# Plain float32 products in place of three split passes for the filters' and long convolutions' transforms

## The chip, the cores and the metric

The kernel runs on one core of a Trainium2 chip. The metric is the device time of one execution in microseconds (us). Three runs of the kernel before took 3001.47, 3002.57 and 3002.89 us, median 3002.57 us. The trace comes from one further, profiled execution, whose own time was 2998.99 us.

A core has a matrix engine (TensorE, PE in the rows; its weight loads are PEld), VectorE (DVE), ScalarE (ACT), GpSimd (POOL) and a queue that issues transfers (SP). Each engine works through its own list of instructions in order.

## The reference, cut to what matters

Two transformer-like blocks run one after the other on a sequence of 512 positions and 1024 channels. The first block has two branches, a linear recurrence (branch A) and a Hyena operator (branch B), then a mixture of 16 experts; the second has four kinds of attention and a feed-forward part. The change is in the Hyena filters and in their long convolutions:

```python
def hyena_filters(L, w1, b1, w2, b2, w3, freq):
    ...
    h = jnp.sin(freq[1] * (h @ w2.astype(f32) + b2.astype(f32)))
    h = (h @ w3.astype(f32)).reshape(L, HYENA_ORDER, 2, HYENA_WIDTH)
    ...
    return h * decay[:, None, None, :]

def fftconv(u, k, bias):
    L = u.shape[1]
    U = jnp.fft.rfft(u, n=2 * L, axis=1)
    K = jnp.fft.rfft(k, axis=0)
    y = jnp.fft.irfft(U * K[None], n=2 * L, axis=1)[:, :L]
    return y + u * bias.astype(jnp.float32)
    ...
        z = v.astype(f32)
        for n, gate in enumerate((x1, x2)):
            k = bidir_kernel(filt[:, n, 0], filt[:, n, 1])
            z = gate.astype(f32) * fftconv(z, k, filt_bias[l, n])
        y_b = z.astype(dt) @ w_b_out[l]
```

## The kernel before, in words

The kernel passes these stages, with the times of the trace: the first norm and the gate of branch A (0 to 58 us); the recurrence of branch A, in whose gaps the Hyena filters are made and transformed (58 to 268 us, `recurrence`, `make_filters`); the output product of branch A (268 to 316 us); branch B (316 to 607 us, `branch_b`); the merge of the branches (607 to 705 us); the experts (705 to 1650 us), paced by their weights' transfers; the second block (1650 to 2997 us).

A float32 operand that goes into a matrix product is split in two: `hi`, a copy rounded to the type float32r (made by ScalarE), and `lo`, the rest, `x - hi` (made by VectorE with a subtraction, L155 in `split`). The product is then three float32r passes into the same PSUM tile (`mm3`, L163 to L165): hi by hi, lo by hi, hi by lo. A matrix product of the experts, the transposes (operand `ident`) and a few small ones take plain float32 operands, with no split.

The transforms use a table `dft` of 2048 columns: 16 blocks of 128 by 128, cosines and sines of a Fourier transform at half-odd frequencies; 8 blocks serve the forward transform and 8 the inverse. It is split once, at the start, into `dft_h` and `dft_l`. A channel quarter `q` (256 of the 1024 channels) and an order `n` (0 or 1) make one filter and one long convolution, eight of each.

- `filters(n, q)` makes a filter's time samples: four products of 512 columns (tiles `fps`), times the decay (`fb`, L1282), each split into `sdh`, `sdl`.
- `filters.transforms` sends them through `transform`: six PSUM tiles of two products each (12 products of 128 by 128 by 256 columns), sums and differences on VectorE (`so`, `sa`, `K`), and stores the spectrum `K` to DRAM.
- `long_conv` transforms the signal (`uh`, `ul`; 8 products), multiplies it with the spectrum (`pq`, `U`, L1358 to L1361), forms sums and differences, and splits the four result tiles into `Yh`, `Yl`. `inverse` then makes 8 products into two tiles `cps`.
- After order 0, `gated` multiplies the result with a gate (`z`, L1411) and splits it into the next `uh`, `ul`. After order 1, `last` transposes the result back and multiplies it into `x` (L1425). `to_operand` makes the first `uh`, `ul` from transposed tiles (L1341, L1342).

So there are 96 products in the filters' transforms, 64 in the signals' forward and 64 in the inverse transforms, three passes each. Between them stand the projections of the input (`acc` from `hh`, `hl` and `wh`, `wl`; 24 passes of 512 columns each, with one split of the weights, `wl`, 128 by 1024 on VectorE, per projection).

The program's steps are written in an order given by two strings (`STEPS_A` for the recurrence, filters and transforms; `STEPS_B` for branch B: c is a projection, u an operand, L a long convolution, M its inverse, G a gate's projection). A scheduler then interleaves the instructions of neighbouring steps in each engine's list; the tiles' buffer counts (`CFG1`) limit how far it goes.

Of the kernel before, what the change touches and what calls it, by code (L numbers as in the profile page):

```python
# [846 lines left out]
CFG1 = dict(acc=3, c=2, f=3, hA=0, lA=1, gh=0, gl=1, hB=0, lB=1, kh=0, kl=1, xh=0, xl=1, sh=0, sl=1, yh=0, yl=1, wl=1, rA=1, rX=1, bl=0, tA=5, tB=5, cv=9, U=3, Y=4, th=5, fA='vvvv', fB='vvvv', gB='vvvv', hB2='vvvv', xg=1, K=1, zh=0, zl=1)  # L847
# [82 lines left out]
def body_t1(c, A):  # L930
# [87 lines left out]
    dft_h = dp.tile([128, 2048], F32R, name="dft_h")  # L1018
    dft_l = dp.tile([128, 2048], F32R, name="dft_l")
    HS = dp.tile([128, T], F32R, name="HS")  # L1020
    HS0 = dp.tile([128, 256], F32R, name="HS0")
    with pool("filt") as fp:
        softplus_cols(c, fp, sp, p1[:, 176:192], 16, -4.0)
        nc.vector.tensor_scalar(spd, sp, 2.0, None, op0=OP.mult)
        filter_mlp(c, A, fp, ps_f, dft_h, dft_l, HS, HS0)
    c.kd = c.dram.tile([8, 128, 4, T], F32, name="filters_dram")
    with pool("lru", 2, side="right") as lp:
        recurrence(c, A, h, proj, lp, ps_c, ps_f, hb, sp, spd, quarter, dft_h, dft_l, HS, HS0)
    with pool("lru2", 2, side="right") as lp:
        branch_a(c, A, h, proj, lp)  # L1030
    with pool("hy", 2, side="right") as bp:
        branch_b(c, A, h, proj, ps_c, ps_f, bp, dft_h, dft_l)
# [40 lines left out]
def filter_mlp(c, A, fp, ps_f, dft_h, dft_l, HS, HS0):  # L1073
# [38 lines left out]
def recurrence(c, A, h, proj, lp, ps_c, ps_f, hb, sp, spd, quarter, dft_h, dft_l, HS, HS0):  # L1112
# [7 lines left out]
    filters = make_filters(c, A, ps_f, t, lp, ws2, dft_h, dft_l, HS, HS0)  # L1120
# [86 lines left out]
def make_transform(c, ps_f, t, dft_h, dft_l, NT, st2):  # L1207
# [40 lines left out]
def make_filters(c, A, ps_f, t, bp, ws, dft_h, dft_l, HS, HS0):  # L1248
    nc = c.nc
    NT = CFG1["tA"]  # L1250
    transform = make_transform(c, ps_f, t, dft_h, dft_l, NT, CFG1["fA"])

    def filters(n, q):
# [10 lines left out]
        sh, sl = t("sdh", 1, F32R, 8 * Q), t("sdl", 1, F32R, 8 * Q)  # L1264
        r = lambda a: a.rearrange("p (g i n) -> p g i n", g=2, i=4)
        for i in range(4):
# [570 lines left out]
```

## Time and profile before

| quantity | value |
|---|---|
| median of three runs | 3002.57 us |
| profiled execution, own time | 2998.99 us |
| its span, first to last instruction | 2997.2 us |
| PE busy | 2789.5 us (93%) |
| PEld busy (weight loads, beside PE) | 1851.5 us (62%) |
| DVE busy | 1595.7 us (53%) |
| ACT busy | 966.0 us (32%) |
| POOL busy | 177.6 us (6%) |
| mean granted TensorE clock | 0.976 of full speed |

The shares are means over stages with different limits, so they say nothing by themselves about one stage. The end of a matrix product in the trace is modelled: one product's duration is longer than its distance to the next one, and this distance is what a product costs in a dense stream. The same holds, less strongly, for VectorE.

A plain float32 product is recorded as two instructions: the 56 plain products at L1736 in pairs of experts, of 128 by 128 by 512 columns, are 112 records.

### The profile page before, as it was taken

The numbers are of one execution on the slowest core, as the hardware profiler recorded it, in microseconds if no ns is written. First come the engines' busy times: TensorE is split into PE (matmuls) and PEld (weight loads), VectorE is DVE, ScalarE is ACT, GpSimd is POOL, SyncE is SP. The second block draws the span as 40 slices with busy tenths as digits, with TensorE's granted clock in tenths as the row PEclk, the third lists the DMA queues.
The fourth block names the chain that finished last, engine by engine and source line by source line (L and its number), as shares of the span: only waits on it lengthen the run. The fifth ranks groups of instructions, "written<-read, shape, count | busy, mean of one in ns | idle before, by whom it ended". The sixth has DMA issues, their size and how long they took to land.

```text
span 2997.2 us, 35639 instructions
## 1 busy us (share of the span) xinstructions
PE 2789.5 (93%) x13524; PEld 1851.5 (62%) x13524; DVE 1595.7 (53%) x3205; ACT 966.0 (32%) x1629; POOL 177.6 (6%) x150
## 2 busy tenths in 40 slices
PE   8898988699999999998988899899999999999998
PEld 7677876575333333333333676688888776688887
DVE  7997599954122222222211889663435788654345
ACT  6774333231000000000000358442223367433224
POOL 0000000000000000000000223200000233100000
PEclk9999998899999999999999899999999999999999
DMA  4344322258999999999999233232222323232324
GB/s 158 130 141 165 120 95 75 98 199 353 417 421 420 420 421 421 421 421 421 420 421 392 89 94 86 64 105 98 94 96 97 119 76 83 76 103 94 99 92 134
DMA packets 136356, 617.94 MB, mean 206 GB/s; under 512 B 17423, under 2 KB 31575, under 8 KB 84600
## 3 DMA queue, kind: packets, MB, share of 16 engines
q1 hardware_dynamic: 136184, 615.65, 54.4%
q8 instruction: 107, 1.75, 0.2%
q14 instruction: 65, 0.53, 0.1%
HBM read 582.03 MB, written 16.78 MB: 200 GB/s over the span
## 4 chain that ended last, share of the span: by engine, by line
PE 64%; DMA 12%; DVE 9%; issue 4%; ACT 1%; POOL 1%; SPq 0%; DVEq 0%; ACTq 0%; POOLq 0%
DMA ew<-experts 12%; PE acc L165 9%; PE acc L164 9%; PE acc L163 9%; PE gps L1684 8%; PE dps L1709 4%; PE S L163 4%; PE S L164 4%; PE S L165 4%; PE o L615 2%; PE acc L1736 2%; PE S L549 2%; PE tp L598 1%; PE acc L1637 1%; DVE wl L155 1%
## 5 line engine op out<-in xcount | busy, mean ns | idle before, releaser
L152 ACT CAST wh<-wr 128x1024 fp32r<-128x1024 f32 (+3 forms) x294 | 291.5, 992 | 793.5 <-PE acc L164 503.4
L1684 PE MATMUL gps<-ew,xe 128*64 128x512 f32 x2048 | 488.8, 597 | 8.8 <-DMA ew<-experts 8.8
L155 DVE TENSOR_TENSOR wl<-wr,wh 128x1024 fp32r<-128x1024 f32 (+3 forms) x291 | 336.2, 1157 | 66.6 <-ACT wh L152 65.7
L1684 PEld LDWEIGHTS gps<-ew,xe 128*64 128x64 f32 x2048 | 151.0, 137 | 285.4 <-issue 253.7
L165 PE MATMUL acc<-hh,wl 128*128 128x512 f32 x768 | 307.1, 401 | 18.0 <-DVE wl L155 17.9
L163 PE MATMUL acc<-hh,wh 128*128 128x512 f32 x768 | 312.2, 406 | 7.2 <-DVE x L1317 3.0
L164 PE MATMUL acc<-hl,wh 128*128 128x512 f32 x768 | 308.6, 402 | 0.0
L1709 PE MATMUL dps<-ew,hT 128*64 128x512 f32 x992 | 224.9, 600 | 15.2 <-DMA ew<-experts 8.8
L164 PE MATMUL acc<-fl,wh 128*128 128x512 f32 (+1 forms) x576 | 213.4, 371 | 0.0
L165 PE MATMUL acc<-fh,wl 128*128 128x512 f32 (+1 forms) x576 | 213.2, 370 | 0.0
L163 PE MATMUL acc<-fh,wh 128*128 128x512 f32 (+1 forms) x576 | 212.9, 370 | 0.0
L165 PE MATMUL S<-hh,wl 128*128 128x512 f32 x512 | 199.9, 391 | 0.0
L164 PE MATMUL S<-hl,wh 128*128 128x512 f32 x512 | 198.9, 389 | 0.0
L163 PE MATMUL S<-hh,wh 128*128 128x512 f32 x512 | 198.9, 389 | 0.0
L1692 DVE TENSOR_TENSOR g<-g,gps 128x512 f32<-128x512 f32 x32 | 21.9, 685 | 330.8 <-PE gps L1684 322.1
L165 PEld LDWEIGHTS acc<-hh,wl 128*128 128x128 f32 x768 | 147.4, 192 | 52.9 <-DVE wl L155 22.3
L163 PEld LDWEIGHTS acc<-hh,wh 128*128 128x128 f32 x768 | 148.0, 193 | 44.8 <-issue 9.4
L1709 PEld LDWEIGHTS dps<-ew,hT 128*64 128x64 f32 x992 | 75.0, 138 | 156.0 <-issue 128.4
L164 PEld LDWEIGHTS acc<-hl,wh 128*128 128x128 f32 x768 | 147.8, 192 | 31.2 <-issue 4.2
L1691 ACT ACTIVATE g<-gps 128x512 f32<-128x512 f32 x32 | 19.2, 599 | 365.7 <-PE gps L1684 353.2
L395 DVE TENSOR_TENSOR x<-acc,x 128x512 f32<-128x512 f32 x56 | 38.8, 692 | 184.1 <-PE acc L165 184.1
L379 DVE SCALAR_TENSOR_TENSOR r<-S,rsb 128x512 f32<-128x512 f32 x64 | 44.1, 692 | 162.4 <-PE S L165 158.7
(422 smaller groups left out, 4740.8 us busy)
## 6 DMA issues: line engine op xcount, KB each, us to landing
ew<-experts SPq DMA_DIRECT2D x384, 1024.0 KB, 19.8
wr<-w_down SPq DMA_DIRECT2D x72, 512.0 KB, 3.3
wr<-w_up SPq DMA_DIRECT2D x64, 512.0 KB, 3.3
wr<-w_in SPq DMA_DIRECT2D x56, 512.0 KB, 3.6
wr<-in_w SPq DMA_DIRECT2D x38, 512.0 KB, 3.4
R<-qkc SPq DMA_DIRECT2D x72, 128.0 KB, 2.3
filters_dram<-K SPq DMA_DIRECT2D x8, 1024.0 KB, 4.5
K<-filters_dram SPq DMA_DIRECT2D x8, 1024.0 KB, 5.0
```

Source lines behind the costliest of these rows:

```text
L152: nc.scalar.copy(hi, src)
L155: (nc.vector if lo_eng == "dve" else nc.gpsimd).tensor_tensor(lo, src, hi.bitcast(F32), op=OP.subtract)
L163: nc.tensor.matmul(ps, W[0], X[0], start=start, stop=False)
L164: nc.tensor.matmul(ps, W[0], X[1], start=False, stop=False)
L165: nc.tensor.matmul(ps, W[1], X[0], start=False, stop=stop)
L379: nc.vector.scalar_tensor_tensor(r, ps, 0.0, rsb, op0=OP.max, op1=OP.mult)
L395: nc.vector.tensor_tensor(x[m], ps, x[m], op=OP.add)
L549: nc.tensor.matmul(ps, q[:, qs], k[:, ks], start=a == 0, stop=a == len(passes) - 1)
L615: nc.tensor.matmul(o[s * 64:(s + 1) * 64, q], v[:, j, vc[s]:vc[s] + 64], pts[s][:, a], start=a == 0, stop=a == len(js) - 1)
L1684: nc.tensor.matmul(ps[h * 64:(h + 1) * 64], xes[e][:, kt], W[:, k, h * T:(h + 1) * T], start=kt == 0, stop=kt == 7)
L1709: nc.tensor.matmul(outs[e][col * 64:(col + 1) * 64], hT[:, j, p * 64:(p + 1) * 64], W[:, p, h * T:(h + 1) * T], start=cc == 0 and j == 0 a ...
L1736: nc.tensor.matmul(ps, Y[f // 4][j][:, (f % 4) * 128:(f % 4 + 1) * 128], st[f // 4], start=j == 0, stop=j == n - 1)
```

## The change

`dft` is loaded straight into one float32 tile and not split. The filters' samples go straight into one float32 tile `fs` (two buffers; before, `sdh` and `sdl` had one each). The signals are one float32 tile `u`, the results of the pointwise product stay in `Z`, from which the inverse reads. Each group of three passes becomes one plain float32 `matmul`. All splits of these operands go. `U` has four buffers instead of three (`Y` with four pairs is gone).

```diff
@@ CFG1
-..., sh=0, sl=1, yh=0, yl=1, ..., U=3, Y=4, ..., zh=0, zl=1)
+..., U=4, u=2, ...)
@@ def filter_mlp
-    raw = fp.tile([128, 2048], F32, name="dft_raw")
-    nc.sync.dma_start(raw, A["dft"])
-    for j in range(4):
-        split(c, raw[:, j * T:(j + 1) * T], dft_h[:, j * T:(j + 1) * T], dft_l[:, j * T:(j + 1) * T])
+    nc.sync.dma_start(dft, A["dft"])
@@ def make_transform
-                mm3(nc, ps[:, half * Q:(half + 1) * Q], (dft_h[:, s], dft_l[:, s]), (v[0][:, r], v[1][:, r]), True, True)
+                nc.tensor.matmul(ps[:, half * Q:(half + 1) * Q], dft[:, s], v[:, r], start=True, stop=True)
@@ def make_filters
-        sh, sl = t("sdh", 1, F32R, 8 * Q), t("sdl", 1, F32R, 8 * Q)
+        fs = t("fs", 2, n=8 * Q).rearrange("p (g i n) -> p g i n", g=2, i=4)
...
-            split(c, s3, r(sh)[:, :, i], r(sl)[:, :, i], hi_eng=ACTDVE[CFG1["sh"]], lo_eng=POOLDVE[CFG1["sl"]])
@@ def branch_b, to_operand
-            nc.scalar.copy(hi[:, :, s], src)
-            nc.vector.tensor_tensor(lo[:, :, s], src, hi[:, :, s].bitcast(F32), op=OP.subtract)
+        by_time(tiles, lambda src, j: nc.scalar.copy(u[:, :, j * 128:(j + 1) * 128], src))
@@ def branch_b, long_conv
-        for r in (0, 2, 1, 3):
-            hi, lo = t("Yh", CFG1["Y"], F32R), t("Yl", CFG1["Y"], F32R)
-            split(c, Z[:, r * T:(r + 1) * T], hi, lo, hi_eng=ACTDVE[CFG1["yh"]], lo_eng=POOLDVE[CFG1["yl"]])
-            out.append((hi, lo))
-        return [out[i] for i in (0, 2, 1, 3)]
+        return Z.rearrange("p (r n) -> p r n", r=4)
@@ def branch_b, inverse
-                    mm3(nc, o, (dft_h[:, w], dft_l[:, w]), (Y[r][0][:, s], Y[r][1][:, s]), half == 0, half == 1)
+                    nc.tensor.matmul(o, dft[:, w], Y[:, r, s], start=half == 0, stop=half == 1)
@@ def branch_b, gated
-            z = t("z1", NT, tag="tmp")
-            nc.vector.tensor_tensor(blocks(z), ps, g[:, s], op=OP.mult)
-            split(c, blocks(z), hi[:, s], lo[:, s], hi_eng=ACTDVE[CFG1["zh"]], lo_eng=POOLDVE[CFG1["zl"]])
+            nc.vector.tensor_tensor(u[:, s], ps, g[:, s], op=OP.mult)
```

The instructions also stand in another order, since the scheduler sees other steps. The first place is the end of branch B on VectorE: the last order-0 convolution's results (L1383, L1384; L1368, L1369 in the changed kernel), the transposed output of the quarter before (`x_93`, `x_94`) and the gate that makes the last signal (`z`, or `u` in the changed kernel). Before:

```order
L1383 TENSOR_TENSOR U<-U 128x2x256
L1384 TENSOR_TENSOR U<-U 128x2x256
L155 TENSOR_TENSOR Yl<-U,Yh 128x512 x4
L1425 TENSOR_TENSOR x_93<-cps,x_3502 128x512
L1425 TENSOR_TENSOR x_94<-cps,x_4657 128x512
L1411 TENSOR_TENSOR z_4717<-cps,xg 128x512
L155 TENSOR_TENSOR ul<-z_4717,uh 128x512
L1411 TENSOR_TENSOR z_4734<-cps,xg 128x512
L155 TENSOR_TENSOR ul<-z_4734,uh 128x512
```

Now:

```order
L1368 TENSOR_TENSOR U<-U 128x2x256
L1369 TENSOR_TENSOR U<-U 128x2x256
L1403 TENSOR_TENSOR x_93<-cps,x_3132 128x512
L1403 TENSOR_TENSOR x_94<-cps,x_4014 128x512
L155 TENSOR_TENSOR wl<-wr,wh 128x1024
L1390 TENSOR_TENSOR u<-cps,xg 128x512 x2
```

Six subtractions are gone from this place, and the split of one projection's weights (`wl`) stands in it.

The second place is the same end of branch B on TensorE, from the last inverse of order 0 to the first product of the merge (`ybh`). Before:

```order
L165 MATMUL acc<-hh,wl 128x512
L1423 MATMUL cps<-ident,U 128x128 x8
L163 MATMUL cps<-Yh,dft_h 128x256
L164 MATMUL cps<-Yl,dft_h 128x256
L165 MATMUL cps<-Yh,dft_l 128x256
...
L1423 MATMUL cps<-ident,U 128x128 x8
L163 MATMUL acc<-ybh,wh 128x512 x2
```

Now:

```order
L163 MATMUL acc<-hh,wh 128x512
L1381 MATMUL cps<-U,dft 128x256 x8
L1213 MATMUL fps<-u,dft 128x256 x8
L164 MATMUL acc<-hl,wh 128x512
L165 MATMUL acc<-hh,wl 128x512
...
L1381 MATMUL cps<-U,dft 128x256 x8
L1401 MATMUL cps<-ident,U 128x128 x8
L163 MATMUL acc<-ybh,wh 128x512 x2
```

Before, 72 passes of transforms (an inverse, a forward transform, an inverse) stand there without any other product between them. Now 20 passes of the last gate's projection (`acc` from `hh`, `hl`) stand between the last forward transform and the last inverse.

## Rows read from the trace of the kernel before

**Rows 1.** Busy time of each engine in stretches of the span, us from its start: the recurrence with the filters, the first part of branch B, two stretches in its middle, its end, and the experts. Columns: stretch, length, busy us (and instructions) of PE, PEld, DVE, ACT, POOL, granted clock, DMA share, GB/s.

```profile
58.00:268.00 210.00, 190.74 (x929) 153.97 (x928) 196.00 (x317) 151.35 (x212) 0.00 (x0) 0.95 0.39 132
316.00:415.00 99.00, 98.36 (x490) 82.78 (x489) 70.57 (x93) 35.96 (x49) 0.00 (x0) 1.00 0.31 103
490.00:508.00 18.00, 5.92 (x30) 4.22 (x29) 17.35 (x24) 4.48 (x8) 0.00 (x0) 0.69 0.13 39
508.00:556.00 48.00, 47.65 (x243) 40.18 (x244) 44.24 (x62) 16.80 (x26) 0.00 (x0) 0.94 0.35 120
556.00:607.00 51.00, 22.42 (x116) 18.54 (x115) 41.21 (x59) 14.88 (x26) 0.26 (x2) 0.73 0.18 64
705.00:1650.00 945.00, 869.37 (x4175) 329.03 (x4173) 208.03 (x701) 61.37 (x103) 14.28 (x33) 0.99 1.00 415
```

**Rows 2.** What TensorE waited for, in the recurrence with the filters (first two rows) and in branch B from 415 to 607 us (last two): us in total, times, longest.

```profile
PE fps L164 <- DVE sdl L155: 4.7, 6, 1.6
PE fps L163 <- ACT sdh L152: 3.2, 2, 1.7
...
PE cps L163 <- ACT Yh L152: 17.0, 2, 16.2
PE acc L165 <- DVE wl L155: 15.9, 2, 8.3
```

**Rows 3.** VectorE's subtractions for the operands of the transforms, by tile and shape: the first row from the recurrence's stretch, the others from branch B. Columns: count, then busy us, mean ns of one, then idle time before them and what ended it.

```profile
L155 DVE TENSOR_TENSOR sdl<-fb,sdh 128x512 fp32r<-128x512 f32 x32 | 20.8, 677 | 0.1
...
L155 DVE TENSOR_TENSOR Yl<-U,Yh 128x512 fp32r<-128x512 f32 x32 | 20.0, 685 | 0.0
...
L155 DVE TENSOR_TENSOR ul<-z,uh 128x512 fp32r<-128x512 f32 x8 | 5.4, 688 | 1.5 <-ACT uh L152 1.4
L1342 DVE TENSOR_TENSOR ul<-cps,uh 128x512 fp32r<-128x512 f32 x8 | 5.3, 688 | 0.1
```

**Rows 4.** Pieces of the chain of work that ended last, in branch B, in order of time: all that are a split's work on the transforms' operands but the last one. Columns: start, us, what. The first `ul` at L1342 has a second one of the same length behind it, the first at L155 too.

```profile
428.41 1.20 DVE Yl L155 x2
...
430.21 1.20 DVE Yl L155 x2
...
450.52 1.04 ACT Yh L152 x2
...
452.05 0.58 DVE Yl L155
...
452.64 1.28 DVE Yl L155 x2
...
459.06 0.60 DVE ul L155
...
499.38 0.60 DVE ul L1342
...
568.65 2.41 DVE Yl L155 x4
...
575.82 0.63 ACT uh L152
576.47 0.69 DVE ul L155
...
577.80 0.63 ACT uh L152
```

**Rows 5.** The timeline of TensorE in a filter's transform, three passes in a row: start, modelled us, instruction.

```profile
85.96 0.28 PE L163 MATMUL fps<-sdh,dft_h 128*128 128x256 f32 x1
86.08 0.28 PE L164 MATMUL fps<-sdl,dft_h 128*128 128x256 f32 x1
86.20 0.28 PE L165 MATMUL fps<-sdh,dft_l 128*128 128x256 f32 x1
```

**Rows 6.** Weight loads: one of a filter's transform, and two of a dense stream of plain float32 products of 512 columns in the experts' stage, between which twelve others stand, one per instruction. Columns: start, us, instruction.

```profile
85.96 0.19 PEld L164 LDWEIGHTS fps<-sdl,dft_h 128*128 128x128 f32 x1
...
839.18 0.19 PEld L1736 LDWEIGHTS acc<-st,Y 128*128 128x128 f32 x1 [0.24 <-issue]
...
844.76 0.19 PEld L1736 LDWEIGHTS acc<-st,Y 128*128 128x128 f32 x1 [0.24 <-issue]
```

**Rows 7.** The timeline of TensorE where one plain float32 product of 512 columns (x2, its two instructions) stands between float32r passes of 512 columns: one that fills the array (L212), and one with 16 of its 128 output rows (L1550). Columns: start, modelled us, instruction.

```profile
29.02 0.39 PE L163 MATMUL acc<-gh,wh 128*128 128x512 f32 x1
29.24 0.39 PE L164 MATMUL acc<-gl,wh 128*128 128x512 f32 x1
29.51 1.12 PE L212 MATMUL bc_ps<-diag,ones 128*128 128x512 f32 x2
...
30.70 0.39 PE L163 MATMUL acc<-gh,wh 128*128 128x512 f32 x1
...
658.32 0.39 PE L163 MATMUL acc<-mh,wh 128*128 128x512 f32 x1
658.63 1.03 PE L1550 MATMUL lps<-x,first 128*16 128x512 f32 x2
...
659.93 0.39 PE L165 MATMUL acc<-mh,wl 128*128 128x512 f32 x1
```

**Rows 8.** TensorE's busy time on the products with `dft_h` (two of the three passes of each transform's product) in four stretches of branch B. Columns: stretch, length, busy us (instructions), granted clock, DMA share, GB/s.

```profile
316.00:415.00 99.00, 12.23 (x60) 1.00 0.31 103
462.00:490.00 28.00, 6.99 (x36) 1.00 0.35 114
508.00:556.00 48.00, 13.43 (x64) 0.94 0.35 120
556.00:607.00 51.00, 12.97 (x48) 0.73 0.18 64
```

More of the change, by code (lines that the diff above doesn't have):

```diff
@@ L1017, in body_t1 @@
     nc.vector.memset(quarter, 0.25)
-    dft_h = dp.tile([128, 2048], F32R, name="dft_h")
-    dft_l = dp.tile([128, 2048], F32R, name="dft_l")
+    dft = dp.tile([128, 2048], F32, name="dft")
     HS = dp.tile([128, T], F32R, name="HS")
@@ L1024, in body_t1 @@
         nc.vector.tensor_scalar(spd, sp, 2.0, None, op0=OP.mult)
-        filter_mlp(c, A, fp, ps_f, dft_h, dft_l, HS, HS0)
+        filter_mlp(c, A, fp, ps_f, dft, HS, HS0)
     c.kd = c.dram.tile([8, 128, 4, T], F32, name="filters_dram")
     with pool("lru", 2, side="right") as lp:
-        recurrence(c, A, h, proj, lp, ps_c, ps_f, hb, sp, spd, quarter, dft_h, dft_l, HS, HS0)
+        recurrence(c, A, h, proj, lp, ps_c, ps_f, hb, sp, spd, quarter, dft, HS, HS0)
     with pool("lru2", 2, side="right") as lp:
@@ L1031, in body_t1 @@
     with pool("hy", 2, side="right") as bp:
-        branch_b(c, A, h, proj, ps_c, ps_f, bp, dft_h, dft_l)
+        branch_b(c, A, h, proj, ps_c, ps_f, bp, dft)
     d_ctx.close()
@@ L1070, in body_t1, with filter_mlp @@
     w_ctx.close()
-def filter_mlp(c, A, fp, ps_f, dft_h, dft_l, HS, HS0):
+def filter_mlp(c, A, fp, ps_f, dft, HS, HS0):
     nc = c.nc
     p1 = c.p1
-    raw = fp.tile([128, 2048], F32, name="dft_raw")
-    nc.sync.dma_start(raw, A["dft"])
-    for j in range(4):
-        split(c, raw[:, j * T:(j + 1) * T], dft_h[:, j * T:(j + 1) * T], dft_l[:, j * T:(j + 1) * T])
+    nc.sync.dma_start(dft, A["dft"])
     z = fp.tile([33, T], F32, name="z")
@@ L1109, in filter_mlp, with recurrence @@
         nc.vector.tensor_scalar(HS0[:, k:k + 1], HS[:, 0:1].bitcast(F32), 0.5, None, op0=OP.mult)
-def recurrence(c, A, h, proj, lp, ps_c, ps_f, hb, sp, spd, quarter, dft_h, dft_l, HS, HS0):
+def recurrence(c, A, h, proj, lp, ps_c, ps_f, hb, sp, spd, quarter, dft, HS, HS0):
     nc, p1 = c.nc, c.p1
@@ L1119, in recurrence @@
     ws2 = WStream(c, lp, 2, 2, size=T, tag="l")
-    filters = make_filters(c, A, ps_f, t, lp, ws2, dft_h, dft_l, HS, HS0)
+    filters = make_filters(c, A, ps_f, t, lp, ws2, dft, HS, HS0)
     def inputs(ct):
@@ L1204, in blocks, with make_transform @@
     return a.rearrange("p (b n) -> p b n", n=Q)
-def make_transform(c, ps_f, t, dft_h, dft_l, NT, st2):
+def make_transform(c, ps_f, t, dft, NT, st2):
     nc = c.nc
@@ L1245, in make_transform, with make_filters @@
     return transform
-def make_filters(c, A, ps_f, t, bp, ws, dft_h, dft_l, HS, HS0):
+def make_filters(c, A, ps_f, t, bp, ws, dft, HS, HS0):
     nc = c.nc
     NT = CFG1["tA"]
-    transform = make_transform(c, ps_f, t, dft_h, dft_l, NT, CFG1["fA"])
+    transform = make_transform(c, ps_f, t, dft, NT, CFG1["fA"])
     def filters(n, q):
@@ L1298, in make_filters, with branch_b @@
     return filters
-def branch_b(c, A, h, proj, ps_c, ps_f, bp, dft_h, dft_l):
+def branch_b(c, A, h, proj, ps_c, ps_f, bp, dft):
     nc, p1 = c.nc, c.p1
@@ L1332, in operand @@
     def operand():
-        return [t(nm, 2, F32R, 4 * Q) for nm in ("uh", "ul")]
+        return blocks(t("u", CFG1["u"], n=4 * Q))
     def to_operand(tiles):
-        hi, lo = [blocks(a) for a in operand()]
-        def put(src, j):
-            s = slice(j * 128, (j + 1) * 128)
-            nc.scalar.copy(hi[:, :, s], src)
-            nc.vector.tensor_tensor(lo[:, :, s], src, hi[:, :, s].bitcast(F32), op=OP.subtract)
-        by_time(tiles, put)
-        return hi, lo
+        u = operand()
+        by_time(tiles, lambda src, j: nc.scalar.copy(u[:, :, j * 128:(j + 1) * 128], src))
+        return u
     def to_gate(tiles):
@@ L1350, in to_gate @@
         return g
-    transform = make_transform(c, ps_f, t, dft_h, dft_l, NT, CFG1["fB"])
+    transform = make_transform(c, ps_f, t, dft, NT, CFG1["fB"])
     def cmul(u, k):
```

19 lines of the change are left out of this document (7 added, 12 removed).

## The prediction

> **What bounds the kernel now.** I read the busy times by stretch first, to see which stages the change can touch. The recurrence with the filters (210 us) has VectorE busy for 196.0 us of it and TensorE for 190.7: two engines near their limit, with a granted clock of 0.95 [rows 1]. Branch B begins with 99 us in which TensorE is busy for 98.4 us. In the middle the roles change: from 490 to 508 us VectorE is busy 17.4 of 18 us while TensorE works 5.9; from 508 to 556 us TensorE works 47.7 of 48 us; at the end, 556 to 607 us, TensorE works 22.4 of 51 us and VectorE 41.2 [rows 1]. The experts behind it run at a DMA share of 1.00 for 945 us [rows 1]; their transfers begin when branch B's and the merge's memory is free, so what is won or lost before them shifts them whole.
>
> Second, the waits of TensorE. In the recurrence 4.7 + 3.2 = 7.9 us are waits for `sdl` and `sdh`, which the change removes; in branch B the long ones are for `Yh` (17.0 us, of which 16.2 us is the one wait for the last convolution's VectorE work, not for the copy itself) and for `wl` (15.9 us), the split of a projection's weights that stands in VectorE's queue behind convolution work [rows 2]. Third, the chain of waits, to see which of the removed work stands on the path in branch B: 2.4 + 4.1 + 1.2 + 4.4 = 12.1 us in four VectorE pieces (415 to 441, 449 to 462, 490 to 508, 556 to 607 us; each second `ul` counted) [rows 4]. Between these pieces the chain runs through TensorE.
>
> **What goes.** 32 subtractions for filters, 32 for `Yl`, 16 for `ul` [rows 3]. Their recorded mean is 677 to 688 ns, but in a row they cost less: four `Yl` take 2.41 us on the chain, 0.60 each [rows 4]. That is 32 x 0.60 = 19.2 us of VectorE in the recurrence and 48 x 0.60 = 28.8 us in branch B, and as many copies on ScalarE (72, since the eight of `to_operand` stay as plain copies). Eight more splits' worth of work for the table goes at the start, where TensorE is dense and the VectorE work lies beside it: I count it at nothing; if that cover is gone it is 4 x 0.60 = 2.4 us.
>
> **What comes: the product.** Three passes of 256 columns stand 0.12 us apart, 0.36 us per product [rows 5]. A plain product of 256 columns fed by a full 128 by 128 weight tile does not occur at full clock. The nearest row is the dense stream at 512 columns: 13 steps from 839.18 to 844.76 us, 0.429 us per instruction, two instructions per product, so 0.86 us [rows 6]. Half the columns gives 0.43 us if all of it scales, more if a fixed part is in it. The bounds are 0.43 and, if nothing scaled, 0.86 us; float32r passes do scale (0.23 us at 512 columns, 0.12 at 256) [rows 5, 7], so I take 0.435: 0.075 us more per product, 16.8 us for 224.
>
> The Trainium skill, page "FP8 and Floating Point Precision", section "TensorE Precision Notes", has true float32 as four passes through the array. By that a product would cost 4/3 of three passes, 0.48 us as an estimate, 0.12 us more each; the row of 0.429 us per instruction lies closer to four times 512 columns without a pass's fixed part, and the measurement decides. By the page the sum below would be some 10 us less favourable, near no change.
>
> The page "TensorE: Matmul & The Clock Gate", section "Weight-path perf modes — Fast Weight Load (FWL) and DoubleRow", says that weights load fast only when the type is not FP32; if float32r counted as such, plain loads would be the new limit. The trace doesn't show it: a load of `dft_h` for float32r and a plain one both take 0.19 us [rows 6].
>
> **What comes: the switch between kinds.** Where one plain product that fills the array stands between passes, the stretch from 29.24 to 30.70 us is 1.46 us; two passes of 0.227 and 0.86 would be 1.31, so the switch costs 0.15 us. With a plain product of 16 output rows it is 658.32 to 659.93, 1.61 us, a switch of 0.30 us [rows 7]. The transforms' products fill the array: I take 0.15, keep 0.30 as the upper bound, and 0 as the lower. In the changed kernel's order the 224 products stand in 53 runs on TensorE, 33 in the recurrence and 20 in branch B.
>
> **The recurrence.** TensorE gets 96 x 0.075 = 7.2 us and 33 x 0.15 = 5.0 us, 12.2 in all. From one side, if all other waiting vanished, the stretch could not be shorter than 190.7 + 12.2 = 202.9 us, 7.1 us less than now. From the other, if only the two named waits go, it is 12.2 - 7.9 = 4.3 us longer. VectorE, which was busy 93% of the stretch, loses a tenth of its work and `fs` has a second buffer, so I go two thirds of the way to the better end: 4.3 - 2/3 x 11.4 = -3.3 us.
>
> **Branch B.** The 12.1 us of splits on the chain go. What is late next in those places is the arithmetic of the convolution itself (`U`, `pq`) and the transposed output (`x`), which stay; the inverse then waits for `Z` instead of `Yl`. Against it, products on TensorE's pieces of the chain: (60 + 36 + 64) / 2 = 80 [rows 8], 80 x 0.075 = 6.0 us; 80/128 of 20 switches, 12.5 x 0.15 = 1.9 us. In the last stretch there are 24, of which the two inverses (16) run largely at half clock (0.73 granted on average) [rows 8], where a product's excess doubles: 16 x 0.15 + 8 x 0.075 = 3.0 us. Together +10.9 us. The products in the VectorE pieces lie in TensorE's idle time.
>
> The order gives back 4.5 us: 20 passes of 0.227 us of a gate's projection stood before the last inverse of order 0, in a stretch with TensorE full [rows 1], and now stand behind the last forward transform, where TensorE waited 16.2 us for VectorE [rows 2]. Their weights' split `wl`, one VectorE instruction, now stands ahead of the gate's `u`; behind it is queued the last convolution, so some 1.2 us of that is lost, within the next term. Last, the 26 or so subtractions off the chain (16 us) made VectorE's queue long when the chain entered it, as the two `wl` waits show [rows 2]. Bounds 0 and -16 us; most of them lie beside full TensorE stretches, so I take -2 us net of that `wl`. Branch B: -12.1 + 10.9 - 4.5 - 2.0 = -7.7 us.
>
> **Sum.** -3.3 - 7.7 = -11.0 us. Against the profiled execution, 2998.99 us (span 2997.2 and 1.8 us around it), that is 2988.0 us. The median of the runs shown is 3.6 us above it, 3002.57, so I predict 2991.6 us, 2992 rounded.
>
> **Rivals.** *VectorE sets the pace throughout.* For it: 196.0 us of 210 busy, and the `wl` waits [rows 1, 2]. Then its whole relief comes off, limited in the recurrence by TensorE's floor: -7.1 - 28.8 = -36 us, 2967 us. Against it: the 99 us at the start of branch B, where TensorE is full and more work comes.
>
> *TensorE takes it all back.* All 128 products of branch B and their switches are paid, 9.6 + 1.2 (half clock) + 3.0 = 13.8 us against 12.1, and the recurrence breaks even: 3004 us, no change. For it: as little as 8 us of idle TensorE is left in the recurrence once 12.2 us come.
>
> *Slower: the switch.* If each switch costs the 0.30 us of the second case in rows 7 and none of the new TensorE work finds idle time, it is 16.8 + 1.2 + 53 x 0.30 = 33.9 us against the 7.9 and 12.1 us of named relief: +13.9, 3016 us. With everything on the path it is slower from (20.0 - 18.0) / 53 = 0.04 us per switch on, so what decides is how much of it meets idle time. For it: plain products stand mostly in runs of two to eight, wherever a PSUM tile comes free, on an engine already busy 91% of the recurrence.
>
> **How the numbers follow.** Forecast 0.47, with its own range 2982 to 2999 (the terms 0 to 0.30 per switch, the recurrence between -7.1 and +4.3); VectorE throughout 0.16; no change 0.22; slower 0.15. A difference under 0.2% (6 us) can't be told from no change here. A slice of the forecast's range lies within that, so faster 0.62, same 0.23, slower 0.15. For 8 times in 10 the range reaches most of the way to the first rival and to the third: 2970 to 3012 us.
>
> **What would show it.** Plain products of 256 columns as pairs of records 0.21 to 0.22 us apart; more shows a fixed part. At the borders of their runs a gap of about 0.1 us. In the recurrence no waits on a split of filter samples, VectorE near 177 us, and the stretch some 207 us long. In branch B the `wl` waits of 15.9 us shrunk, TensorE at work in the last convolution's VectorE time, and its stretch near 283 us. The experts' stretch must stay at 945 us. I am wrong if TensorE is full through all of branch B (then no gain), if the weight loads of plain products show beside their 0.19 us a wait of their own, or if a new wait on a free `U` or `u` buffer takes the place of `Yh`.

## The result and the profile after

The changed kernel takes 2968.76 us (median of 4 runs, 2967.63 to 2970.56), the kernel before beside it 3002.73 us: ratio 0.9889, 95% interval 0.9876 to 0.9901. By the medians that is 34.0 us faster. The forecast was 2992 us; the time lies 1.2 us below the range's lower end and within 2 us of the first rival, "VectorE sets the pace throughout" (2967 us). The profiled execution took 2967.98 us, 31.0 us less than before's. In later series two of five runs of `after_again` and one of four of `plain_fewer_buffers` were disturbed and took 3213.78 us or more; what is given for these two kernels is over their other runs.

| stage, by the first product of the next | before | after | forecast of the change | measured |
|---|---|---|---|---|
| start, until the recurrence | 58.3 | 59.6 | 0 | +1.3 |
| recurrence with the filters | 210.1 | 197.3 | -3.3 | -12.8 |
| branches A and B | 336.8 | 314.4 | -7.7 | -22.4 |
| merge, until the experts' first product | 117.4 | 120.2 | 0 | +2.8 |
| experts and second block | 2274.6 | 2274.7 | 0 | +0.1 |

The merge took 117.4 to 120.6 us among the kernels run, those with before's products included, with a granted clock of 0.99 to 0.94; its +2.8 us is not shown to be the change's. The start's +1.3 us goes with it: the recurrence begins at 56.6 to 59.1 us in every kernel run that splits the table or half of it, and at 59.6 to 61.2 us in every one that does not. Why, no run shows; the prediction had counted this split at nothing. The page's busy times of the changed kernel: over the whole span TensorE is about as busy as before (2789.5 us), although its 160 forward and 64 inverse products became dearer, and VectorE 50 us less.

```profile
span 2966.2 us, 35028 instructions
## 1 busy us (share of the span) xinstructions
PE 2792.8 (94%) x13300; PEld 1849.3 (62%) x13300; DVE 1546.1 (52%) x3121; ACT 922.6 (31%) x1553; POOL 177.6 (6%) x150
```

Busy time by stretch, of the changed kernel (recurrence; branches A and B; then branch B cut where TensorE first waits). Columns as in [rows 1].

```profile
59.60:256.90 197.30, 188.08 (x834) 150.80 (x833) 178.52 (x285) 131.91 (x179) 0.00 (x0) 0.99 0.42 140
256.90:571.30 314.40, 287.57 (x1265) 235.00 (x1265) 235.79 (x313) 84.91 (x117) 0.26 (x2) 0.95 0.34 114
...
305.60:362.00 56.40, 56.40 (x258) 47.05 (x257) 28.25 (x34) 18.77 (x25) 0.00 (x0) 1.00 0.35 117
362.00:571.30 209.30, 183.44 (x814) 149.37 (x812) 188.38 (x256) 54.26 (x78) 0.26 (x2) 0.93 0.28 96
```

The same view of the kernel before, cut at the same events:

```profile
58.30:268.40 210.10, 190.47 (x930) 153.98 (x929) 196.31 (x317) 151.47 (x212) 0.00 (x0) 0.95 0.39 132
268.40:605.20 336.80, 284.85 (x1393) 236.12 (x1393) 265.54 (x362) 107.49 (x157) 0.26 (x2) 0.91 0.32 108
...
317.00:381.00 64.00, 64.00 (x301) 53.63 (x300) 37.22 (x46) 20.52 (x27) 0.00 (x0) 1.00 0.30 103
381.00:605.20 224.20, 173.30 (x897) 143.71 (x896) 208.23 (x292) 74.98 (x116) 0.26 (x2) 0.88 0.27 90
```

The experts' products, first to last start, in the kernel before and in the changed kernel (count, ns of one as least, median and most, then the two starts in us):

```profile
L1684 PE MATMUL gps<-ew,xe x2048: 592/592/1061, 722.6 to 1634.5; 128*64 128x512 f32 x187
```

```profile
L1662 PE MATMUL gps<-ew,xe x2048: 592/592/1061, 691.5 to 1603.2; 128*64 128x512 f32 x187
```

The experts take as long as before (911.9 and 911.7 us), 31 us earlier.

Three things are to be seen. VectorE lost 17.8 us of work in the recurrence and 29.8 us in the branches, and the stages got shorter by 72% and 75% of that. Once branch B's first projections are done, VectorE is busy 93% of the remaining 224 us before and 90% of 209 us after: that it sets the pace there, and not the 12.1 us of splits on the chain [rows 4] alone, the experiments below show. And TensorE's busy time in the two stages is the same in the two kernels (190.47 + 284.85 = 475.32 us before, 188.08 + 287.57 = 475.65 after), while its idle time fell from 71.58 to 36.05 us, by 35.5 us: that is what the two stages gained (35.2). The dearer products add next to no busy time, since the granted clock rose from 0.95 to 0.99 and from 0.91 to 0.95: by the clock's record in the traces, TensorE was busy at its lower level (1.2 instead of 2.4 GHz) for 41.1 us of these stages before and for 22.5 us after.

What TensorE waited for in the changed kernel (picked rows), in the recurrence (first two rows) and in the branches (last two), where [rows 2] had 7.9 us on the splits, 17.0 us on `Yh` and 15.9 us on `wl`:

```profile
PE fps L1264 <- DVE fs L1276: 2.2, 1, 2.2
PE fps L1213 <- DVE fs L1276: 1.4, 2, 0.9
...
PE cps L1381 <- DVE U L1365: 12.3, 1, 12.3
PE acc L165 <- DVE wl L155: 11.9, 2, 6.9
```

The price of a plain product, on TensorE's timeline. Each run of plain products (x4 is two products) is followed by one pass of 512 columns and then the next pass; the starts of the run and of that next pass are compared. Columns: start, modelled us, instruction.

```profile
84.67 1.02 PE L1213 MATMUL fps<-fs,dft 128*128 128x256 f32 x4
85.35 0.58 PE L164 MATMUL acc<-hl,wh 128*128 128x512 f32 x1
85.77 0.39 PE L165 MATMUL acc<-hh,wl 128*128 128x512 f32 x1
86.00 0.39 PE L163 MATMUL acc<-hh,wh 128*128 128x512 f32 x1
...
106.43 1.89 PE L1213 MATMUL fps<-fs,dft 128*128 128x256 f32 x8
107.97 0.58 PE L164 MATMUL acc<-hl,wh 128*128 128x512 f32 x1
108.39 0.39 PE L163 MATMUL acc<-hh,wh 128*128 128x512 f32 x1
...
412.01 3.62 PE L1381 MATMUL cps<-U,dft 128*128 128x256 f32 x16
415.28 0.58 PE L164 MATMUL acc<-hl,wh 128*128 128x512 f32 x1
415.69 0.39 PE L163 MATMUL acc<-hh,wh 128*128 128x512 f32 x1
```

Two products and a pass take 1.10 us, four and a pass 1.96, eight and a pass 3.68: 0.43 us per product. With the pass's 0.23 us (85.77 to 86.00) only 1.10 - 0.86 - 0.23 = 0.01 us is left for the switch there and back. Of the 53 runs, 39 stand at full clock, without a recorded wait and with a 512-column pass behind them; worked out in the same way, 24 of these leave 0.02 us or less, the others 0.03 to 0.40 us, and the mean is 0.05 us. The product was forecast right (0.435), the switch (0.15) was not; why the two products of [rows 7] left 0.15 and 0.30 us is not shown. The four passes that the Trainium skill states (page "FP8 and Floating Point Precision", section "TensorE Precision Notes") would give 0.48 us as an estimate by three passes' 0.36; the measured 0.43 us decides.

### The profile page after: what moved, and what is told of

Read it like the earlier page. It is cut to its first block, busy times and chain, and to the rows that moved or that the text cites. A ratio compares the mean times of both kernels' runs of the same rounds, so it can differ in the third digit from the quotient of the medians.

```text
span 2966.2 us, 35028 instructions
## 1 busy us (share of the span) xinstructions
PE 2792.8 (94%) x13300; PEld 1849.3 (62%) x13300; DVE 1546.1 (52%) x3121; ACT 922.6 (31%) x1553; POOL 177.6 (6%) x150
## 4 chain that ended last, share of the span: by engine, by line
PE 71%; DVE 11%; DMA 11%; issue 4%; ACT 2%; POOL 1%; SPq 0%; DVEq 0%; ACTq 0%; POOLq 0%
PE acc L165 10%; PE acc L164 10%; PE acc L163 10%; PE gps L1662 9%; DMA ew<-experts 9%; PE dps L1687 5%; PE S L163 4%; PE S L164 4%; PE S L165 4%; PE fps L1213 2%; PE o L615 2%; PE acc L1615 1%; PE S L549 1%; DVE wl L155 1%; PE acc L1714 1%
## 5 line engine op out<-in xcount | busy, mean ns | idle before, releaser
L155 DVE TENSOR_TENSOR wl<-wr,wh 128x1024 fp32r<-128x1024 f32 (+3 forms) x291 | 336.3, 1156 | 69.5 <-ACT wh L152 68.8
L163 PE MATMUL acc<-hh,wh 128*128 128x512 f32 x768 | 312.5, 407 | 0.8 <-ACT wh L152 0.5
L163 PE MATMUL S<-hh,wh 128*128 128x512 f32 x512 | 198.9, 389 | 0.0
L1670 DVE TENSOR_TENSOR g<-g,gps 128x512 f32<-128x512 f32 x32 | 21.9, 685 | 331.0 <-PE gps L1662 322.2
L163 PEld LDWEIGHTS acc<-hh,wh 128*128 128x128 f32 x768 | 147.3, 192 | 38.6 <-issue 6.7
L1669 ACT ACTIVATE g<-gps 128x512 f32<-128x512 f32 x32 | 19.2, 599 | 365.8 <-PE gps L1662 353.4
```

The source lines that it names most:

```text
L155: (nc.vector if lo_eng == "dve" else nc.gpsimd).tensor_tensor(lo, src, hi.bitcast(F32), op=OP.subtract)
L163: nc.tensor.matmul(ps, W[0], X[0], start=start, stop=False)
```

## The experiments

Every kernel ran beside the kernel before on its chip; times are medians. R is the recurrence's time and B that of branches A and B, from the profile of each run (before 210.1 and 336.8, after 197.3 and 314.4).

**Is it the splits or the kind of product?** `three_nosplit` keeps three passes and leaves the low parts of the samples and signals out, `plain_extra_sub` keeps VectorE's work.

```diff
@@ three_nosplit: changed kernel, with dft_h, dft_l made as before
-  nc.tensor.matmul(ps[...], dft[:, s], v[:, r], start=True, stop=True)
+  mm3(nc, ps[...], (dft[0][:, s], dft[1][:, s]), (v[:, r].bitcast(F32R), v[:, r].bitcast(F32R)), True, True)
... (the inverse likewise)
@@ plain_extra_sub: changed kernel, make_filters
+            j3 = t("junk", 1).rearrange("p (g n) -> p g n", g=2)
+            nc.vector.tensor_tensor(j3, fs[:, :, i], fs[:, :, i], op=OP.subtract)
... (likewise at the three other places of a former split)
```

> The changed kernel's data flow with three float32r passes per product again (table split, operands only rounded by the instruction that makes them: their low part is left out, the middle pass repeats the rounded operand). VectorE and ScalarE work as in the changed kernel, TensorE work as before. If the gain is VectorE's relief and TensorE's dearer products are partly paid, this is faster than the changed kernel, by up to 224 x 0.073 = 16 us: 2953 to 2966 us. If the gain came from plain products on TensorE in any way, it is back near 3000 us. If TensorE's excess is wholly hidden, 2966 to 2971 us.

Measured: 2969.53 us, ratio 0.9887 (0.9872 to 0.9901); R 200.5, B 315.2.

> The changed kernel with the 80 subtractions of 128 x 512 put back on VectorE at their old places, each into a scratch tile that nobody reads; nothing waits for them but VectorE's queue. If VectorE's time is what the gain comes from, most of the 34 us goes: 2990 to 3010 us (above 3003 if TensorE's dearer products are then paid on top). If the gain is the shorter dependence (no copy, no subtraction between producer and product) or the buffers, it stays at 2965 to 2980 us.

Measured: 3010.74 us, ratio 1.0024 (1.0013 to 1.0035); R 214.4, B 336.3. So the gain is VectorE's time: without the 80 subtractions three passes and plain products run equally long (2969.5 and 2968.8 us), with them neither gains (3001.5 us for before on that chip, and 3010.7). Nor is it ScalarE's copies or the shorter way from producer to product: `plain_extra_sub` goes without these copies and waits too, and gains nothing. Busy time by stretch, recurrence and branches, first of `three_nosplit`, then of `plain_extra_sub`:

```profile
58.10:258.60 200.50, 185.19 (x930) 151.20 (x929) 178.23 (x285) 133.34 (x180) 0.00 (x0) 0.97 0.40 138
258.60:573.80 315.20, 279.58 (x1393) 232.32 (x1393) 235.88 (x313) 84.25 (x117) 0.26 (x2) 0.94 0.35 118
```

```profile
61.10:275.50 214.40, 191.01 (x833) 153.29 (x832) 194.52 (x314) 132.59 (x179) 0.00 (x0) 0.96 0.38 127
275.50:611.80 336.30, 292.29 (x1264) 236.49 (x1264) 266.97 (x364) 85.19 (x117) 0.26 (x2) 0.92 0.32 110
```

TensorE of `three_nosplit` executes as many instructions as before's (930 and 1393) and is busy 464.8 instead of 475.3 us, with the granted clock at 0.97 for 0.95 and 0.94 for 0.91. It was busy at the lower level for 24.2 us instead of 41.1; what takes 16.9 us there takes half of that at the full level, so some 8.4 of the 10.5 us are the clock's by this estimate, and the rest is not separated. The plain products of the changed kernel put 10.9 us of busy time back (475.7), and its idle time is 14.9 us less than here (36.0 for 15.3 + 35.6 us): they lie in waits.

**Each half alone.** `filters_only` leaves three passes in branch B, `convs_only` in the filters.

```diff
@@ filters_only (in branch_b) / convs_only (in make_filters): both tables are kept
-    transform = make_transform(c, ps_f, t, dft, NT, ...)
+    transform = make_transform3(c, ps_f, t, *c.dft3, NT, ...)
... (with the splits of that half as before)
```

> Only the filters' transforms are plain; the long convolutions keep three passes and their splits. The traces show the recurrence 12.8 us shorter: if the parts are independent, 2987 to 2992 us with the recurrence at 197 to 199 us. By the terms of the prediction, -3.3 us: 2999 us.

Measured: 2990.58 us, ratio 0.9956 (0.9941 to 0.9971); R 197.8, B 338.7.

> Only the long convolutions are plain; the filters keep three passes and their splits. The traces show branch B 22 us shorter: if the parts are independent, 2978 to 2984 us with the recurrence at 209 to 211 us. By the terms of the prediction, -7.7 us: 2995 us.

Measured: 2992.77 us, ratio 0.9967 (0.9954 to 0.9979); R 226.2, B 310.4. Each half shortens its own stage by about what the whole change does (R -12.3, B -26.4). But the untouched recurrence of `convs_only` takes 16 us more than before's, with the same work in another order, and the whole misses its 2978 to 2984 us. The two halves alone gain 10.9 and 8.7 us, together they gain 34: what one half is worth in the whole is not read from these runs.

**The order of the work.** That made the recurrence's 12.8 us doubtful, so the recurrence's list of steps was disturbed in both kernels (branch B's was not).

```diff
@@ before_order_1, after_order_1, convs_only_order: STEPS_A
-... r2 i4 ... r4 G2 i6 ...
+... i4 r2 ... r4 i6 G2 ...
@@ before_order_2, after_order_2: STEPS_A
-... r3 i5 ... G4 f5 t5 ...
+... i5 r3 ... f5 t5 G4 ...
```

> The same work as the kernel before; two neighbouring steps of the recurrence's list trade places twice, which moves some 1,000 lines of TensorE's order there. Theory 'VectorE's time': the recurrence stays within 4 us of the 210.1 us of before, and the whole at 2998 to 3007 us. Rival 'the order of the work': by the order alone the recurrence moves by 8 us or more (convs_only's moved by 16 us), and the whole with it.

> The changed kernel with the same two trades as before_order_1. Theory 'VectorE's time': recurrence 194 to 201 us, whole 2965 to 2973 us, and 9 us or more below before_order_1's recurrence. Rival 'the order of the work': recurrence anywhere from 195 to 225 us.

Measured: 3007.51 us (R 210.3, B 338.7) and 2971.18 us (R 196.3, B 315.3).

> The same work as the kernel before, another two trades in the same list. Theory 'VectorE's time': recurrence 206 to 214 us, whole 2998 to 3007 us. Rival 'the order of the work': 8 us or more away from 210.1 us, to either side, and if below 200 us then before's own order was an unlucky one.

> The changed kernel with the trades of before_order_2. Theory 'VectorE's time': recurrence 194 to 201 us, whole 2965 to 2973 us, and 9 us or more below before_order_2's. Rival 'the order of the work': anywhere from 195 to 225 us, and no steady difference between the two pairs.

Measured: 3011.73 us (R 212.6, B 338.4) and 2973.13 us (R 198.4, B 314.4). The pairs differ by 36.3 and 38.6 us, R by 14.0 and 14.2: the gain does not hang on one order. (Both orders of before took longer than the 3007 us expected at most, by 0.5 and 4.7 us.)

> convs_only with two neighbouring steps of the recurrence's list traded twice, as in before_order_1; the work is the same. Theory 'convs_only's 226 us were its order's, with TensorE at the lower clock for part of it': recurrence 207 to 216 us, whole 2974 to 2986 us. Rival 'something of convs_only itself (the second table, the buffers) slows the recurrence': 222 us or more, whole 2989 us or more.

Measured: 2991.98 us; R 218.7, B 316.2. R lies between the two expectations, the whole with the rival (2989 us or more): by the order R got 7.5 us shorter, but B 5.8 us longer, and 219 us is still more than any order of before. Part of the oddity can be read. The recurrence of `convs_only`, and its TensorE's timeline (passes of one filter before, in and behind a slow stretch):

```profile
58.10:284.30 226.20, 199.07 (x932) 159.90 (x931) 201.39 (x323) 150.81 (x213) 0.00 (x0) 0.92 0.38 127
```

```profile
95.91 0.39 PE L164 MATMUL fps<-sdl,dft_h 128*128 128x256 f32 x1 [1.15 <-DVE sdl L155]
96.13 0.28 PE L165 MATMUL fps<-sdh,dft_l 128*128 128x256 f32 x1
96.25 0.30 PE L163 MATMUL fps<-sdh,dft_h 128*128 128x256 f32 x1
...
99.56 0.41 PE L164 MATMUL fps<-sdl,dft_h 128*128 128x256 f32 x1
99.77 0.41 PE L165 MATMUL fps<-sdh,dft_l 128*128 128x256 f32 x1
...
115.92 0.28 PE L163 MATMUL fps<-sdh,dft_h 128*128 128x256 f32 x1
116.04 0.28 PE L164 MATMUL fps<-sdl,dft_h 128*128 128x256 f32 x1
```

Half a microsecond behind a wait of 1.15 us for a split, the passes' distance goes from 0.12 to 0.21 us, and at 110 us it is back at 0.12: from 96.4 to 110.0 us TensorE runs at the lower level of its clock, 1.2 instead of 2.4 GHz (granted 0.50 there, 0.92 over this recurrence). So waits are paid twice, once as idle time and once as slow passes behind them: of the 16 us more than before's recurrence, 7.5 us are idle time of TensorE (27.1 for 19.6) and 8.6 us busy time for the same passes (199.1 for 190.5). Why this kernel meets more such waits stays open.

**How much each engine is worth.** Four kernels change one engine's load in the changed kernel.

```diff
@@ plain_sub_filters: scratch subtraction at the filters alone
+            nc.vector.tensor_tensor(j3, fs[:, :, i], fs[:, :, i], op=OP.subtract)
@@ plain_gates_nosplit: gates of the recurrence, WStream.get
+        if lo_eng == "none":
+            c.nc.scalar.copy(hi, raw)
+            lo = hi
...
-            c.gate(n, lp, ..., lo_eng=POOLDVE[CFG1["gl"]])
+            c.gate(n, lp, ..., lo_eng="none")
@@ one_pass
-  nc.tensor.matmul(o, dft[:, w], Y[:, r, s], ...)
+  nc.tensor.matmul(o, dft[0][:, w], Y[:, r, s].bitcast(F32R), ...)
@@ plain_pool_gates: CFG1
-gl=1
+gl=0
```

> The changed kernel with one scratch subtraction of 128x512 behind each of the 32 filter blocks, whose result nothing reads. Theory 'VectorE's time in the recurrence': recurrence back up by 10 to 18 us, to 207 to 215 us, branches A and B unchanged at 313 to 317 us, whole 2978 to 2988 us. Rival 'the split counted because the products waited for it': recurrence within 4 us of 197.3 us, whole 2966 to 2974 us.

Measured: 2996.24 us, ratio 0.9981 (0.9971 to 0.9990); R 213.6, B 318.9. The 32 subtractions cost R 16.3 us although no product waits for their results: VectorE's occupancy, not a product's wait for the result, is what counts here. The whole lies above the 2978 to 2988 us expected; B, where nothing was changed, is 4.5 us longer, and that is not explained.

> The changed kernel without the low parts of the gate weights of the recurrence (the third pass takes the high part again): twelve VectorE subtractions of 128x1024, some 14 us by 1.16 us each, are gone and nothing goes to GpSimd; TensorE's passes are as many as before. Theory 'VectorE's time still sets the recurrence's pace': recurrence 5 to 11 us shorter, 186 to 192 us, whole 2957 to 2964 us. Rival 'after the change TensorE's passes set it': TensorE is busy 188 of the 197 us, so within 3 us of 197.3 us.

Measured: 2970.48 us; R 196.4, B 313.3. VectorE's busy time in the recurrence fell to 167.0 us (ten subtractions fewer, not the twelve expected) and R stayed: the rival held.

> The changed kernel with each plain product replaced by a single float32r pass over rounded operands (the two passes with the low parts are left out of the computation). TensorE's work shrinks by about 224 x (0.435 - 0.12) = 70 us, VectorE's is unchanged. Theory 'VectorE's time sets the pace of the recurrence and branch B': TensorE waits longer instead, the recurrence stays at 190 to 198 us, branches A and B at 300 to 315 us, the whole at 2945 to 2969 us. Rival 'TensorE's passes set the pace after the change': 35 to 70 us go, the whole at 2900 to 2935 us.

Measured: 2953.78 us, ratio 0.9842 (0.9826 to 0.9859); R 190.7, B 306.2. Some 70 us less work for TensorE, an estimate by the passes' distances (in R and B it is busy 52 us less, at a lower granted clock), is worth 15 us. Busy time in the recurrences of `plain_sub_filters`, `plain_gates_nosplit` and `one_pass`:

```profile
60.30:273.90 213.60, 190.27 (x834) 152.56 (x833) 194.60 (x314) 132.46 (x179) 0.00 (x0) 0.96 0.38 127
```

```profile
61.20:257.70 196.50, 188.29 (x834) 152.14 (x833) 166.99 (x275) 131.34 (x179) 0.00 (x0) 0.98 0.42 143
```

```profile
58.90:249.60 190.70, 169.21 (x738) 132.82 (x737) 174.28 (x280) 132.78 (x180) 0.00 (x0) 0.93 0.43 146
```

With VectorE at 195 us (first row) the stage takes 214 us, VectorE's time and its own gaps. At 178 us (changed kernel) TensorE, 188 of 197 us, is the limit, and VectorE at 167 us (second row) helps no more. With TensorE at 169 us (third row) the stage still takes 191, with VectorE busy 174. So the change took the recurrence to about where the two meet.

> The changed kernel with the low parts of the gate weights of the recurrence (12 tiles of 128x1024) subtracted on GpSimd (2.4 us each there) instead of VectorE (1.16 us each): some 14 us less of VectorE's 178 us in the recurrence. Theory 'VectorE's time still sets the recurrence's pace': recurrence 4 to 10 us shorter, whole 2957 to 2966 us. Rival 'after the change something else sets it': within 2 us of 197.3 us, or longer, whole 2966 us or more.

Measured: 2983.54 us, ratio 0.9938 (0.9921 to 0.9956); R 207.4, B 315.7. R is 10 us longer: the rival's "or longer", of a size that it did not name. VectorE has ten subtractions less and is busier, 183.7 instead of 178.5 us. Picked groups of the recurrence, of the changed kernel and of this one (count, busy us, mean ns), then two instructions of this one (start, us):

```profile
L1276 DVE TENSOR_TENSOR fs<-fps,dec 128x512 f32<-128x512 f32 x32 | 21.0, 676 | 0.3 <-DMA dec<-decay 0.3
L1239 DVE TENSOR_TENSOR K<-so 128x512 f32<-128x512 f32 x8 | 5.5, 682 | 0.0
L1161 DVE TENSOR_TENSOR x<-x,th 128x512 f32<-128x512 f32 x8 | 5.4, 676 | 0.0
```

```profile
L1276 DVE TENSOR_TENSOR fs<-fps,dec 128x512 f32<-128x512 f32 x32 | 21.1, 677 | 4.9 <-DMA dec<-decay 4.8
L1161 DVE TENSOR_TENSOR x<-x,th 128x512 f32<-128x512 f32 x8 | 9.1, 1139 | 0.0
L1239 DVE TENSOR_TENSOR K<-so 128x512 f32<-128x512 f32 x8 | 7.6, 955 | 0.0
L1236 DVE TENSOR_TENSOR K<-sa 128x512 f32<-128x512 f32 x8 | 5.5, 682 | 0.0
...
L155 POOL TENSOR_TENSOR wl<-wr,wh 128x1024 fp32r<-128x1024 f32 x10 | 26.5, 2652 | 222.6 <-ACT wh L152 209.6 <-PE fps L1273 13.1
```

```profile
237.78 2.39 POOL L155 TENSOR_TENSOR wl<-wr,wh 128x1024 fp32r<-128x1024 f32 x1 [13.07 <-PE fps L1273]
238.38 2.33 DVE L1161 TENSOR_TENSOR x<-x,th 128x512 f32<-128x512 f32 x1
```

VectorE's instructions with two inputs in SBUF that meet one of GpSimd's subtractions (2.65 us each) mostly get longer: `x` goes from 676 to 1139 ns on average, `K<-so` of L1239 from 682 to 955. The `x` shown takes 2.33 us and ends 0.5 us behind GpSimd's subtraction. `K<-sa` never meets one and stays at 682, and `fs`, which reads `fps` from PSUM, keeps 677. The Trainium skill has this rule (page "SBUF — State Buffer", section "SBUF: two separate sides"): GpSimd and a VectorE instruction with two SBUF inputs contend for one pair of ports, and the one that starts first holds it for its whole instruction. The trace agrees: 26.5 us of GpSimd cost VectorE more than the work it was spared. That is 5.2 of R's 10 us; VectorE also idles 4.8 us more, and the rows of `fs` put 4.6 us of that down to the transfer of `dec` (4.9 for 0.3). Why that came later is not shown.

**The change's side effects.**

```diff
@@ plain_fewer_buffers
-..., U=4, ...; fs = t("fs", 2, ...)
+..., U=3, ...; fs = t("fs", 1, ...)
@@ plain_gates_first: STEPS_B
-... Ga L31 M31 Ge Gc G9 Gd
+... Ga Ge Gc G9 Gd L31 M31
```

> The changed kernel with before's numbers of buffers (three tiles U instead of four, one tile fs instead of two); TensorE's order is that of the changed kernel. If the extra buffers carry none of the gain: 2966 to 2973 us, stages as in the changed kernel. Rival 'the buffers are part of the gain': recurrence or branch B 5 us or more longer, 2974 us or above.

Measured: 2971.16 us; R 198.6, B 313.7. The extra buffers carry nothing that can be seen.

> The changed kernel with the last transform of the list (L31, and M31 behind it) set behind the gates, so that some twenty projection passes no longer lie in the wait of branch B's tail. The prediction put those passes at 4.5 us. Theory 'the moved passes fill a wait': branches A and B 3 to 6 us longer, whole 2971 to 2976 us. Rival 'they make no difference, TensorE has other work there': within 1.5 us of the changed kernel's 2968.8 us.

Measured: 2977.71 us; R 198.9, B 316.9, which is 3.2 us above `plain_fewer_buffers` on the same chip. The moved passes do fill a wait, for somewhat less than the 4.5 us of the prediction. The whole is 6.6 us above `plain_fewer_buffers`, above the 2976 us expected; in the two profiled executions it is 4.3 us, of which 1.0 lies in the merge. What is beyond B's 3.2 us is not explained.

**A version beyond the change.** The recurrence's own gate products get the same treatment.

```diff
@@ plain_gate_products: recurrence
-        split(c, xa, xh, xl, ...)
-        W = ws2.get(A["lru_w"][ct], 4, 128, ...)
-                mm3(nc, ps, (W[0][:, 2 * d + g], W[1][:, 2 * d + g]), (xh, xl), True, True)
+        nc.sync.dma_start(W.rearrange("p (k n) -> p k n", k=4), A["lru_w"][ct])
+                nc.tensor.matmul(ps, W[:, (2 * d + g) * 128:(2 * d + g + 1) * 128], xa, start=True, stop=True)
```

> The changed kernel with the 32 products of the recurrence's own gates (cps<-xh,wh and so on) as plain float32 too: the subtractions of xl and of their weights go (16 of 0.60 us, 9.6 us of VectorE, and as many copies of ScalarE), TensorE gets 32 x (0.87 - 0.70) = 5.4 us more by the price of two halves of 0.436 us. Theory 'VectorE's time first': recurrence 2 to 6 us shorter, whole 2962 to 2968 us. Rival 'TensorE is the bound there by now': 0 to 5 us longer, whole 2969 to 2975 us.

Measured: 2966.41 us, ratio 0.9884 (0.9869 to 0.9899); R 195.9, B 312.5. R fell by 1.4 us, less than the 2 us expected at least. Too close to tell, so both ran side by side:

> The changed kernel once more, to stand beside plain_gate_products_again on one chip: 2966 to 2973 us, ratio to before 0.988 to 0.990.

> plain_gate_products once more. If the recurrence's 1.4 us and the branches' 2 us of its first profile are the kernel's own: 2 to 5 us below after_again. Rival 'no difference that can be measured, since TensorE has no wait left to fill in the recurrence': within 2 us of after_again.

Measured: the changed kernel 2970.92 us, ratio 0.9899 (0.9881 to 0.9917), R 199.1, B 313.7; `plain_gate_products` 2964.35 us, ratio 0.9879 (0.9865 to 0.9892), R 195.6, B 312.4. The intervals overlap, but its four runs (2962.8 to 2967.8) all lie below the three that count for the other (2970.6 to 2976.0), by 6.6 us in the medians. In the profiles R and B are 4.7 us shorter, but the experts and the second block, which are the same in both kernels, 6.7 us too. So it is likely faster than the changed kernel, by some microseconds, and this is not settled.

## Why the prediction was wrong, point by point

The step that failed is the worth of VectorE's relief: the prediction put it at the splits on one chain of waits in branch B, and at the waits for `sdl` and `sdh` and part of the way to a floor in the recurrence. The runs showed that the stages got shorter by 72 and 75% of the time taken from VectorE, and that subtractions which no product waits for cost as much. Two smaller steps failed beside it: the switch, and TensorE's busy time taken as fixed. With 0.01 to 0.05 us for the switch the prediction's own sums give some -8.0 to -6.7 us for the recurrence and -9.5 to -9.0 for branch B, together at most half of the 35.2 us measured.

- *What goes* was right: 19.2 and 28.8 us of VectorE forecast, 17.8 and 29.8 us less busy.
- *The product* was right: 0.43 us measured, 0.435 taken.
- *The switch* was mis-sized: 0.15 us taken from one product in [rows 7], 0.01 measured at most places and 0.05 on average. The 53 runs cost some 0.5 to 2.5 instead of 8 us. Rival three's 0.30 us per switch was not met on average.
- *The recurrence* (-3.3, measured -12.8). The floor was worked out as TensorE's 190.7 us plus the new work, as if that busy time were fixed. With 0.01 us per switch it is 190.7 + 7.2 + 0.3 = 198.2, and the measured 197.3 us is below it, because 190.7 us contained slow passes: at 0.99 instead of 0.95 the dearer work took 188.1 us (16.6 us of TensorE's work there lay at the lower level before, 3.4 after). And "two thirds of the way" had no row behind it; the stage went all the way to TensorE's limit.
- *Branch B* (-7.7, measured -22.4 with branch A). Here the relief was taken as 12.1 us read from the chain plus 2.0 us for the queue, out of 28.8. The chain names one path; beside it stand others nearly as long, it seems, since on an engine that is 93% busy the instructions off the chain counted too. `plain_extra_sub` puts the 48 subtractions, off every path, at 336.3 - 314.4 = 21.9 us. Their bound of -16 us stood in the text and was passed over because "most of them lie beside full TensorE stretches". The full stretch at the start of branch B did not resist: it was 64.0 us with 301 recorded instructions before and 56.4 with 258 after, mainly because 35 passes of the projections (261 before, 226 after) moved behind it, where TensorE had been waiting.
- *TensorE's +10.9 us in branch B* was paid on the chain in the forecast. Plain products instead of three passes do add 8.0 us of busy time there (287.6 for the 279.6 of `three_nosplit`), but they met idle time: B is 314.4 us and 315.2. With VectorE's load kept (`plain_extra_sub`) the kernel is slower than before, ratio 1.0024; of the 12.9 us between the two profiled executions (3011.86 and 2998.99 us) 4.3 lie in the recurrence and none in B (336.3 for 336.8), and the rest, outside, is not explained. That is the sign of rivals two and three, in a kernel that gives VectorE no relief.
- *The first rival* met the time (2967 us), not the parts: it had -7.1 and -28.8 us for the two stages, -12.8 and -22.4 were measured, and the start and the merge took some 4 us back. Its mechanism, VectorE's pace, is the one that the runs show; that the sum fits to 2 us is luck.
- *Two slips in its sums* changed nothing: in the second rival 210.0 - 202.9 = 7.1 us of idle TensorE are left, not 8; and the terms named for the forecast's own range add up to some 2983 to 3001 us, not 2982 to 2999.
- *What would show it*: no waits on splits, VectorE near 177 us (178.5), the weight loads at their 0.19 us (median of the plain products') and the experts as long as before (911.9 and 911.7 us) came as said; the recurrence at 207 us and branch B at 283 us (265.7 after from branch A's last product on, 288.2 before by the same cut) did not. The wait for `Yh` became one for `U` (12.3 us), the convolution's arithmetic, as forecast.

## What to carry to other kernels

First ask of each stage which engine is over 90% busy outside the stretches that another engine fills; what is taken from that engine can be worth most of its own time (here 72 to 75%), wherever it stands, until the next engine's limit is reached. The chain of waits gave a lower end for this here, not the value. Work traded onto an engine that waits cost nothing here, and such a trade can be tested by its halves: take the relief without the new work, and the new work without the relief.

## What the runs showed of the hardware

- TensorE's busy time depends on its waits: the same 2323 instructions were busy 475.3 us with 71.6 us of idle time and 464.8 us with 50.9 us, as the granted clock rose from 0.95 to 0.97 and from 0.91 to 0.94.
- A plain float32 product of 128 by 128 by 256 columns costs 0.43 us at full clock, three float32r passes 0.36 us.
- Going from float32r passes to plain float32 products of a full 128 by 128 tile and back costs 0.01 us at most of 39 places, 0.05 us on average.
- Ten subtractions moved from VectorE to GpSimd (2.65 us each there) left VectorE 5.2 us busier than with them, since instructions of its with two inputs in SBUF got longer beside them (`x` 1139 for 676 ns), and the recurrence 10 us longer.
